# Matmul minus a matrix: transfers of up to eight row tiles in a listed order, through two rings

## The chip, the core and the metric

The kernel runs on one core of a Trainium2 chip. The engines that matter are PE (TensorE, matmuls and transposes by matmul), DVE (VectorE), ACT (ScalarE), SP (which only issues DMA transfers here) and the core's 16 DMA engines, which move data between HBM and the on-chip memory SBUF. Each engine has its own instruction queue and works through it in order; the engines wait for one another through semaphores. PSUM is the memory into which PE writes.

The metric is device time in microseconds (us). Four runs of the kernel before gave 212.73 to 213.39, median 213.12.

## The reference

```python
batch, m, k, n = 16, 512, 1024, 768
x          # (batch, m, k) float32
weight     # (k, n)        float32
sub_value  # (batch, m, n) float32

def reference(x, weight, sub_value):
    return (np.matmul(x, weight) - sub_value).astype(np.float32)
```

Batch and m together are 8192 rows of x. A row of x has 4 KB, a row of `sub_value` or of the output 3 KB. In all 33.6 MB of x, 25.2 MB of `sub_value` and 3.1 MB of weights are read, and 25.2 MB are written.

## The kernel before

**Tiles.** The rows are cut into 64 m tiles of 128 rows, one row to each of the 128 partitions of SBUF. Which row goes where is set by the views `x_s`, `sub_s` and `out_s`: the rows fall into sections of 1024, and in a section partition p holds the S = 8 consecutive rows 8p to 8p + 7. Tile `mi` takes row `mi % 8` of each partition's run in section `mi // 8`. So a transfer of four tiles reads four neighbouring rows for each partition, 16 KB of x or 12 KB of sub in one piece, and the pieces of neighbouring partitions lie 32 KB (x) or 24 KB (sub, out) apart in HBM.

**One tile's way.** ACT casts a tile of x to float16 (`cast`, lines 99 to 108; line 108 for most tiles, 105 for the pairs named below). PE transposes it in four pieces, taking two float16 values as one float32 (`transposes`, line 116), and ACT copies the result out of PSUM (line 123). PE multiplies with the weights in 16 matmuls, four for each of four chunks of k (`matmuls`, line 149). DVE subtracts: `finish` (line 160) reads PSUM and the sub tile and writes the output over the sub tile, from where it is stored. For seven pairs of tiles (18 and 19, 24 and 25, and so on to 54 and 55, `ON_DVE`) DVE does the transpose instead of PE, 16 instructions to a pair (line 137).

**Order.** The program order is written out by hand. A head (lines 186 to 214) does tiles 0 to 2 chunk by chunk as the weights come in, with idle matmuls between. Then a loop over `mi` from 3 to 63 does, in each pass: the transfers (below), the matmuls of tile `mi` with the transposes of tile `mi + 2` between them, the casts of later tiles, `finish(mi)`, and some of the waiting DVE transposes. A tile is cast four passes ahead of its matmuls, a tile of a DVE pair seven passes ahead (`lead`).

**Transfers.** All are issued by SP, in program order. The head's are listed in `HEAD_TRANSFERS`: x and sub one tile at a time at first, then two, with the four weight loads among them. From there on, every fourth pass of the loop issues three transfers of four tiles: a load of x three groups ahead, a load of sub two groups ahead, and the store of the group that was finished two groups ago (lines 220 to 226). After the loop come the last stores: four tiles, then two, one and one (lines 242 to 246).

**Buffers.** A group of four x tiles has a buffer of its own out of four (`x_pool`, 64 KB per partition). A group of four sub tiles, which becomes the output, has one out of seven (`so_pool`, 84 KB per partition); the weights' float32 stages use the same seven. A load into a buffer waits until its previous content is used up: for x until it is cast, for sub until it is stored. Waits are kept by the part of a buffer that an instruction touches: in the profile cast(0) starts when x0 has landed, with loads into other parts of the same buffer under way.

PSUM has two buffers for transposes (`psum_t`) and three for the products (`psum_o`).

Of the kernel before, what the change touches and what calls it, by code (L numbers as in the profile page):

```python
# [8 lines left out]
P = 128  # L9
Q = 32  # L10
F32 = mybir.dt.float32
F16 = mybir.dt.float16

S = 8
G = 4
XA, SA, OA = 3, 2, 2
TA = 2
CA = 2
LEAD_DVE = 7
PER = 4  # L20
HEAD = 3
ON_DVE = frozenset(range(18, 60, 6))
HEAD_TRANSFERS = [('x', 0, 1), ('w', 0, 0), ('x', 1, 1), ('w', 1, 0), ('x', 2, 1), ('w', 2, 0), ('w', 3, 0), ('x', 3, 1), ('s', 0, 1), ('x', 4, 1), ('s', 1, 1), ('x', 5, 1), ('s', 2, 1), ('x', 6, 1), ('s', 3, 1), ('x', 7, 1), ('x', 8, 2), ('s', 4, 2), ('x', 10, 2), ('s', 6, 2)]


@with_exitstack
def kernel(
# [7 lines left out]
    nc = tc.nc  # L35
    keep = tc.keep_in_program_order
# [5 lines left out]
    M_TOT, K = x_flat.shape  # L42
    _, N = weight.shape
    n_mt = M_TOT // P
    n_g = n_mt // G
    NS = N // 2
    KW = K // 2
    n_c = KW // P

    x_s = x_flat.rearrange("(s p j) k -> s p j k", p=P, j=S)  # L50
    sub_s = sub_flat.rearrange("(s p j) n -> s p j n", p=P, j=S)
    out_s = out_flat.rearrange("(s p j) n -> s p j n", p=P, j=S)
    w_c = weight.rearrange("(c p r) n -> c p r n", p=P, r=2)

    def rows(view, mi, n):
        return view[mi // S][:, mi % S : mi % S + n]

    const_pool = ctx.enter_context(tc.tile_pool(name="const", bufs=1))
    w_pool = ctx.enter_context(tc.tile_pool(name="w_pool", bufs=1))
    x_pool = ctx.enter_context(tc.tile_pool(name="x_pool", bufs=4))  # L60
    x16_pool = ctx.enter_context(tc.tile_pool(name="x16_pool", bufs=CA + 2))
    xt_pool = ctx.enter_context(tc.tile_pool(name="xt_pool", bufs=TA + 3))
    x16p_pool = ctx.enter_context(tc.tile_pool(name="x16p_pool", bufs=2))
    xtp_pool = ctx.enter_context(tc.tile_pool(name="xtp_pool", bufs=2))
    so_pool = ctx.enter_context(tc.tile_pool(name="so_pool", bufs=7))
    psum_t_pool = ctx.enter_context(tc.tile_pool(name="psum_t", bufs=2, space=bass.MemoryType.PSUM))
    psum_o_pool = ctx.enter_context(tc.tile_pool(name="psum_o", bufs=3, space=bass.MemoryType.PSUM))

# [3 lines left out]

    w_sb = w_pool.tile([P, n_c, 2, N], F16)

    x_t, so_t, x16_t, xt_t, ps_t, po_t = {}, {}, {}, {}, {}, {}

    def load_w(c):
        st = so_pool.tile([P, 2, N], F32, name="w_stage", tag="so_tile")
        keep(nc.sync.dma_start(out=st, in_=w_c[c]))  # L79
        for r in range(2):  # L80
            keep(nc.vector.tensor_copy(out=w_sb[:, c, r], in_=st[:, r]))  # L81

    def load_x(mi, n):
        g, j = divmod(mi, G)
        if j == 0:
            x_t[g] = x_pool.tile([P, G, K], F32, name="x_tile")
        keep(nc.sync.dma_start(out=x_t[g][:, j : j + n], in_=rows(x_s, mi, n)))  # L87

    def load_sub(mi, n):
        g, j = divmod(mi, G)  # L90
        if j == 0:
            so_t[g] = so_pool.tile([P, G, N], F32, name="so_tile")
        keep(nc.sync.dma_start(out=so_t[g][:, j : j + n], in_=rows(sub_s, mi, n)))

    def store(mi, n):
        g, j = divmod(mi, G)
        keep(nc.sync.dma_start(out=rows(out_s, mi, n), in_=so_t[g][:, j : j + n]))

    def cast(mi):
        g, j = divmod(mi, G)  # L100
        first = mi - mi % 2
        if first in ON_DVE:
            if mi == first:
                x16_t["pair", mi] = x16p_pool.tile([P, 2, K], F16, name="x16p_tile")
            keep(nc.scalar.copy(out=x16_t["pair", first][:, mi - first], in_=x_t[g][:, j]))  # L105
            return
        x16_t[mi] = x16_pool.tile([P, K], F16, name="x16_tile")
        keep(nc.scalar.copy(out=x16_t[mi], in_=x_t[g][:, j]))  # L108


    def transposes(mi):
        def one(c):
            def f():
                if c == 0:
                    ps_t[mi] = psum_t_pool.tile([P, K], F16, name="psum_t")
                keep(nc.tensor.transpose(  # L116
                    ps_t[mi].bitcast(F32)[:, c * P : (c + 1) * P],
                    x16_t[mi].bitcast(F32)[:, c * P : (c + 1) * P],
                    ident,
                ))  # L120
                if c == n_c - 1:
                    xt_t[mi] = xt_pool.tile([P, K], F16, name="xt_tile")
                    keep(nc.scalar.copy(out=xt_t[mi], in_=ps_t.pop(mi)))  # L123
                    x16_t.pop(mi)
            return f
        return [one(c) for c in range(n_c)]

    def transposes_dve(mi):

        x16 = x16_t.pop(("pair", mi)).bitcast(F32).rearrange("p j (c q) -> p (j c) q", c=n_c)  # L130
        xt_p = xtp_pool.tile([P, 2, K], F16, name="xtp_tile")
        xt_t[mi], xt_t[mi + 1] = xt_p[:, 0], xt_p[:, 1]
        xt = xt_p.bitcast(F32).rearrange("p j (c m) -> p (j c) m", c=n_c)

        def one(a, b):
            def f():
                keep(nc.vector.transpose(  # L137
                    xt[b * Q : (b + 1) * Q, :, a * Q : (a + 1) * Q],
                    x16[a * Q : (a + 1) * Q, :, b * Q : (b + 1) * Q],
                ))  # L140
            return f
        return [one(a, b) for a in range(P // Q) for b in range(P // Q)]

    def matmuls(mi, c):
        if c == 0:
            po_t[mi] = psum_o_pool.tile([P, 2, 512], F32, name="psum_o")
        for r in range(2):
            for h in range(2):
                keep(nc.tensor.matmul(  # L149
                    po_t[mi][:, h, :NS],  # L150
                    xt_t[mi][:, 2 * P * c + r : 2 * P * (c + 1) : 2],
                    w_sb[:, c, r, h * NS : (h + 1) * NS],
                    start=(c == 0 and r == 0),
                    stop=(c == n_c - 1 and r == 1),
                ))

    def finish(mi):
        g, j = divmod(mi, G)
        o = so_t[g][:, j].rearrange("p (h n) -> p h n", h=2)
        keep(nc.vector.tensor_tensor(  # L160
            out=o, in0=po_t.pop(mi)[:, :, :NS], in1=o, op=mybir.AluOpType.subtract
        ))


    for kind, at, n in HEAD_TRANSFERS:
        {"w": lambda: load_w(at), "x": lambda: load_x(at, n), "s": lambda: load_sub(at, n)}[kind]()


    idle_w = const_pool.tile([P, P], F16)
# [9 lines left out]
    def lead(mi):  # L179
        return LEAD_DVE if mi - mi % 2 in ON_DVE else TA + CA  # L180
# [4 lines left out]

    idle(13)
    cast(0)
    transpose_tile(0)
    idle(5)
    matmuls(0, 0)  # L190
    cast(1)
    transpose_tile(1)
    idle(4)
    matmuls(0, 1)
    matmuls(1, 0)
    matmuls(1, 1)
    cast(2)
    transpose_tile(2)
    idle(3)
# [6 lines left out]
    for mi in range(HEAD):  # L206
        matmuls(mi, 3)
        finish(mi)
# [7 lines left out]

    waiting = []
    for mi in range(HEAD, n_mt):
        g, j = divmod(mi, G)
        if j == 0 or mi == HEAD:  # L220
            if g + XA < n_g:
                load_x((g + XA) * G, G)
            if g + SA < n_g:
                load_sub((g + SA) * G, G)
            if g >= OA:
                store((g - OA) * G, G)
        t = mi + TA
        tr = transposes(t) if t < n_mt and t - t % 2 not in ON_DVE else []
        for c in range(n_c):
            matmuls(mi, c)  # L230
            if tr:
                tr[c]()
        for t in range(mi, n_mt):
            if t - lead(t) == mi:
                cast(t)
        finish(mi)
        if mi + LEAD_DVE - 1 in ON_DVE:
            waiting += transposes_dve(mi + LEAD_DVE - 1)
        for f in waiting[:PER]:
            f()  # L240
        del waiting[:PER]
    for g in range(n_g - OA, n_g - 1):
        store(g * G, G)
    store(n_mt - G, G - 2)
    store(n_mt - 2, 1)
    store(n_mt - 1, 1)


# [28 lines left out]
```

## Time and profile before

One execution was profiled. It took 212.96 us; the profile's span, from the first to the last instruction, is 211.2 us of it.

| what | value |
|---|---|
| time, median of four runs | 213.12 us |
| time of the profiled execution, its span | 212.96 us, 211.2 us |
| mean granted clock of PE | 0.991 |
| moved between HBM and SBUF | 61.87 MB read, 25.17 MB written |
| transfers issued by SP | 65 |
| matmul of 384 columns (line 149) | 1024 instructions, 326 ns mean, overlapping |
| transposes by PE (line 116) | 200 |
| cast of a tile by ACT (lines 108 and 105) | 64, 1049 and 1046 ns |
| copy of a transposed tile by ACT (line 123) | 50, 1012 ns |
| subtraction by DVE (line 160) | 64, 957 ns |
| transpose by DVE (line 137) | 112, 436 ns |
| last matmul ends, last store issued | 203.9 us, 204.9 us |

Busy time of an engine is what its instructions cover. Matmuls are pipelined, so their times overlap and a busy PE need not be a PE at its peak. The page also divides the span into 40 slices of 5.28 us and gives for each the busy share of every engine and of the DMA engines, in tenths, and the GB/s that were moved. A separate view lists for every line what it waited for, in us in total, in how many cases, and the longest. The chain of waits follows the work that ended last back in time, from each instruction to what released it. For DMA transfers the trace has the time of issue on SP's queue and the time until the data has landed.

### The profile page before, as it was taken

What the parts mean: (1) busy time and instruction counts of PE and PEld (TensorE: products, weight loads), DVE (VectorE), ACT (ScalarE), POOL (GpSimd) and SP (SyncE); (2) the same over time, 40 slices, a digit from 0 to 9 for tenths busy, and PEclk for the clock granted to TensorE, in tenths of its full rate; (3) what the DMA queues carried; (4) which work ended last, traced back from release to release, by engine and by line L of the source; (5) the groups of instructions that cost most, each with busy time, mean ns of one, the idle gap of its engine ahead of it and who ended that gap; (6) DMA issues with size and microseconds to landing.
All of it is one profiled execution on the core that took longest, in us unless ns stands there. A gap on an engine that the chain in (4) does not pass through costs nothing.

```text
span 211.2 us, 3028 instructions
## 1 busy us (share of the span) xinstructions
PE 198.4 (94%) x1249; PEld 130.0 (62%) x1249; DVE 114.1 (54%) x186; ACT 112.6 (53%) x115; POOL 0.7 (0%) x6
## 2 busy tenths in 40 slices
PE   7999799999999999999989999998999999999960
PEld 2465576677666666666656567664656667667630
DVE  0333313152697299399519939942993993242330
ACT  3547666757852846565086555509646453656300
POOL 1000000000000000000000000000000000000000
PEclk9999999999999999999999999999999999999996
DMA  6999999999999999999999999999999999999994
GB/s 217 423 412 391 422 417 446 417 417 441 425 428 417 433 432 414 437 426 431 421 431 434 417 431 429 431 421 432 430 424 433 400 434 414 427 412 431 431 413 182
DMA packets 9374, 87.23 MB, mean 413 GB/s; under 512 B 1040, under 2 KB 1040, under 8 KB 3728
## 3 DMA queue, kind: packets, MB, share of 16 engines
q1 hardware_dynamic: 9360, 87.04, 98.3%
q8 instruction: 10, 0.16, 0.3%
q14 instruction: 4, 0.03, 0.0%
HBM read 61.87 MB, written 25.17 MB: 412 GB/s over the span
## 4 chain that ended last, share of the span: by engine, by line
DMA 49%; PE 33%; ACT 10%; DVE 3%; SPq 2%; issue 1%; ACTq 0%
DMA x_tile<-in_x_dram 49%; PE psum_o L149 28%; PE psum_t L116 5%; ACT x_tile L108 4%; ACT xt_tile L123 3%; ACT x16p_tile L105 2%; DVE xtp_tile L137 2%; DVE so_tile L160 1%; SPq L79 1%; SPq L87 1%; ACTq L105 0%
## 5 line engine op out<-in xcount | busy, mean ns | idle before, releaser
L149 PE MATMUL psum_o<-w_sb,xt_tile 128*128 128x384 f16 x800 | 145.7, 326 | 1.7 <-ACT xt_tile L123 1.6
L149 PEld LDWEIGHTS <-xt_tile 128*128 128x128 f16 x800 | 78.2, 98 | 41.6 <-ACT xt_tile L123 2.7
L160 DVE TENSOR_TENSOR so_tile<-psum_o,so_tile 128x768 f32<-128x768 f32 x64 | 60.8, 957 | 57.2 <-PE psum_o L149 33.7
L123 ACT COPY xt_tile<-psum_t 128x1024 f16<-128x1024 f16 x50 | 50.6, 1012 | 58.9 <-PE psum_t L116 58.2
L137 DVE STREAM_TRANSPOSE xtp_tile<-x16p_tile 32x256 f32<-32x256 f32 x112 | 48.8, 436 | 22.4 <-ACT x16p_tile L105 20.6
L108 ACT CAST x_tile<-x_tile 128x1024 f16<-128x1024 f32 x50 | 51.7, 1049 | 6.7 <-DMA x_tile<-in_x_dram 6.6
L116 PE MATMUL psum_t<-ident,x_tile 128*128 128x128 f32 x200 | 52.4, 274 | 2.0 <-ACT x_tile L108 1.4
L149 PE MATMUL psum_o<-w_sb,xtp_tile 128*128 128x384 f16 x224 | 42.9, 326 | 0.6 <-DVE xtp_tile L137 0.6
L116 PEld LDWEIGHTS psum_t<-ident,x_tile 128*128 128x128 f32 x200 | 27.6, 141 | 16.1 <-ACT x_tile L108 4.3
L149 PEld LDWEIGHTS <-xtp_tile 128*128 128x128 f16 x224 | 21.8, 98 | 10.9 <-DVE xtp_tile L137 1.4
L105 ACT CAST x16p_tile<-x_tile 128x1024 f16<-128x1024 f32 x14 | 14.6, 1046 | 20.9 <-DMA x_tile<-in_x_dram 20.9
L81 DVE CAST w_sb<-w_stage 128x768 f16<-128x768 f32 x8 | 4.1, 556 | 10.3 <-DMA w_stage<-in_weight_dram 10.3
L177 PE MATMUL psum_o<-idle_x,idle_w 128*128 128x512 f16 x25 | 8.4, 493 | 1.3 <-DVE idle_x L172 1.3
L177 PEld LDWEIGHTS <-idle_w 128*128 128x128 f16 x25 | 3.1, 122 | 4.9 <-issue 3.2
L108 ACT ACT_TABLE_LOAD x1 | 1.3, 1283 | 0.7 <-PEq L261 0.7
L171 DVE MEMSET idle_w<- 128x64 uint32 x1 | 0.1, 112 | 0.8 <-PEq L261 0.8
masks.py:199 POOL TENSOR_SCALAR_AFFINE_SELECT ident<-ident 128x128 f32<-128x128 f32 x1 | 0.3, 295 | 0.1
L172 DVE MEMSET idle_x<- 128x256 uint32 x1 | 0.3, 272 | 0.0
masks.py:197 POOL MEMSET ident<- 128x128 f32 x1 | 0.2, 205 | 0.3 <-POOLq L261 0.3
L261 POOL MEMSET const-bfloat16-1.0<- 128x1 bf16 x1 | 0.1, 102 | 0.0
L261 POOL MEMSET const-uint8-127<- 128x1 uint8 x1 | 0.1, 102 | 0.0
L261 POOL MEMSET const-float32-0.0<- 128x1 f32 x1 | 0.1, 99 | 0.2 <-issue 0.2
(1 smaller groups left out, 0.1 us busy)
## 6 DMA issues: line engine op xcount, KB each, us to landing
x_tile<-in_x_dram SPq DMA_DIRECT2D x13, 2048.0 KB, 30.8
out_dram<-so_tile SPq DMA_DIRECT2D x15, 1536.0 KB, 31.7
so_tile<-in_sub_value_dram SPq DMA_DIRECT2D x14, 1536.0 KB, 32.9
x_tile<-in_x_dram SPq DMA_DIRECT2D x8, 512.0 KB, 10.7
w_stage<-in_weight_dram SPq DMA_DIRECT2D x4, 768.0 KB, 8.5
x_tile<-in_x_dram SPq DMA_DIRECT2D x2, 1024.0 KB, 13.0
so_tile<-in_sub_value_dram SPq DMA_DIRECT2D x4, 384.0 KB, 11.8
so_tile<-in_sub_value_dram SPq DMA_DIRECT2D x2, 768.0 KB, 13.6
```

The source lines that it names most:

```text
L79: keep(nc.sync.dma_start(out=st, in_=w_c[c]))
L81: keep(nc.vector.tensor_copy(out=w_sb[:, c, r], in_=st[:, r]))
L87: keep(nc.sync.dma_start(out=x_t[g][:, j : j + n], in_=rows(x_s, mi, n)))
L105: keep(nc.scalar.copy(out=x16_t["pair", first][:, mi - first], in_=x_t[g][:, j]))
L108: keep(nc.scalar.copy(out=x16_t[mi], in_=x_t[g][:, j]))
L116: keep(nc.tensor.transpose(ps_t[mi].bitcast(F32)[:, c * P : (c + 1) * P], x16_t[mi].bitcast(F32)[:, c * P : (c + 1) * P], ident,))
L123: keep(nc.scalar.copy(out=xt_t[mi], in_=ps_t.pop(mi)))
L137: keep(nc.vector.transpose(xt[b * Q : (b + 1) * Q, :, a * Q : (a + 1) * Q], x16[a * Q : (a + 1) * Q, :, b * Q : (b + 1) * Q],))
L149: keep(nc.tensor.matmul(po_t[mi][:, h, :NS], xt_t[mi][:, 2 * P * c + r : 2 * P * (c + 1) : 2], w_sb[:, c, r, h * NS : (h + 1) * NS], start ...
L160: keep(nc.vector.tensor_tensor(out=o, in0=po_t.pop(mi)[:, :, :NS], in1=o, op=mybir.AluOpType.subtract))
L177: keep(nc.tensor.matmul(idle_o[:, 0], idle_w, idle_x, start=True, stop=True))
L261: nc = _bacc.Bacc("TRN2", target_bir_lowering=False, num_devices=1)
```

## The change

The views keep their form, but S is 64 instead of 8: partition p now holds rows 64p to 64p + 63 of x, `sub_value` and the output, and the whole input is one section. Tile `mi` is row `mi` of each partition's run. In HBM the pieces of neighbouring partitions lie 256 KB (x) or 192 KB (sub, out) apart, and a transfer of eight tiles takes 32 KB or 24 KB in one piece for each partition.

The groups of four are gone. One tile of SBUF with 16 slots holds x (64 KB per partition, as before), one with 32 slots holds sub and output (96 KB per partition); tile `mi` sits in slot `mi % 16` or `mi % 32`. The weights' float32 stages use the last eight slots of the second ring.

All transfers stand in one list, `TRANSFERS`, which SP issues in that order. `issue()` is called once at the start and then after every `cast` and every `finish` while the program is built; it places the next entries of the list as long as what they need has been placed: for a load of x the casts of the tiles that had its slots, for a load of sub the stores of those tiles, for a store the finishes of its tiles. On the chip each transfer then waits for these to be done. The list begins with x0, the weights and single tiles, goes on with two to five tiles, and has transfers of eight from sub 8 to 15 on. It has 39 entries.

What is computed, and the order of work on PE, ACT and DVE, stay as they are.

```diff
-S = 8
-G = 4
-XA, SA, OA = 3, 2, 2
+S = 64
+NX, NSO = 16, 32
...
+TRANSFERS = [
+    ('x', 0, 1), ('w', 0, 1), ('x', 1, 1), ('w', 1, 1), ('x', 2, 1), ('w', 2, 1),
+    ('w', 3, 1), ('x', 3, 2), ('s', 0, 1), ('x', 5, 3), ('s', 1, 3), ('x', 8, 3),
+    ('s', 4, 4), ('x', 11, 5), ('s', 8, 8), ('x', 16, 8), ('x', 24, 3), ('s', 16, 8),
+    ('x', 27, 5), ('o', 0, 8), ('s', 24, 8), ('x', 32, 8), ('s', 32, 8), ('o', 8, 8),
+    ('x', 40, 8), ('s', 40, 8), ('x', 48, 8), ('o', 16, 8), ('o', 24, 8), ('s', 48, 8),
+    ('x', 56, 8), ('s', 56, 8), ('o', 32, 8), ('o', 40, 8), ('o', 48, 8), ('o', 56, 4),
+    ('o', 60, 2), ('o', 62, 1), ('o', 63, 1),
+]
...
+    x_ring = x_pool.tile([P, NX, K], F32)
+    so_ring = so_pool.tile([P, NSO, N], F32)
...
+    def issue():
+        while todo:
+            kind, at, n = todo[0]
+            span = set(range(at, at + n))
+            old = {t - NX if kind == "x" else t - NSO for t in span}
+            need, by = {
+                "w": (set(), "o"),
+                "x": ({t for t in old if t >= 0}, "cast"),
+                "s": ({t for t in old if t >= 0}, "o"),
+                "o": (span, "finish"),
+            }[kind]
+            if not need <= done[by]:
+                return
+            todo.pop(0)
+            done[kind] |= span
...
+            here = ring[:, at % size : at % size + n]
+            there = view[at // S][:, at % S : at % S + n]
+            if kind == "o":
+                keep(nc.sync.dma_start(out=there, in_=here))
+            else:
+                keep(nc.sync.dma_start(out=here, in_=there))
...
     def cast(mi):
...
+        issue()
...
     def finish(mi):
...
+        issue()
...
     for mi in range(HEAD, n_mt):
-        g, j = divmod(mi, G)
-        if j == 0 or mi == HEAD:
-            if g + XA < n_g:
-                load_x((g + XA) * G, G)
-            if g + SA < n_g:
-                load_sub((g + SA) * G, G)
-            if g >= OA:
-                store((g - OA) * G, G)
...
-    for g in range(n_g - OA, n_g - 1):
-        store(g * G, G)
-    store(n_mt - G, G - 2)
-    store(n_mt - 2, 1)
-    store(n_mt - 1, 1)
```

More of the change, by code (lines that the diff above doesn't have):

```diff
@@ L22 @@
 ON_DVE = frozenset(range(18, 60, 6))
-HEAD_TRANSFERS = [('x', 0, 1), ('w', 0, 0), ('x', 1, 1), ('w', 1, 0), ('x', 2, 1), ('w', 2, 0), ('w', 3, 0), ('x', 3, 1), ('s', 0, 1), ('x', 4, 1), ('s', 1, 1), ('x', 5, 1), ('s', 2, 1), ('x', 6, 1), ('s', 3, 1), ('x', 7, 1), ('x', 8, 2), ('s', 4, 2), ('x', 10, 2), ('s', 6, 2)]
+TRANSFERS = [
[7 rows of a table added]
+]
 @with_exitstack
@@ L44 @@
     n_mt = M_TOT // P
-    n_g = n_mt // G
     NS = N // 2
@@ L59 @@
     w_pool = ctx.enter_context(tc.tile_pool(name="w_pool", bufs=1))
-    x_pool = ctx.enter_context(tc.tile_pool(name="x_pool", bufs=4))
+    x_pool = ctx.enter_context(tc.tile_pool(name="x_pool", bufs=1))
     x16_pool = ctx.enter_context(tc.tile_pool(name="x16_pool", bufs=CA + 2))
@@ L64 @@
     xtp_pool = ctx.enter_context(tc.tile_pool(name="xtp_pool", bufs=2))
-    so_pool = ctx.enter_context(tc.tile_pool(name="so_pool", bufs=7))
+    so_pool = ctx.enter_context(tc.tile_pool(name="so_pool", bufs=1))
     psum_t_pool = ctx.enter_context(tc.tile_pool(name="psum_t", bufs=2, space=bass.MemoryType.PSUM))
@@ L73 @@
     w_sb = w_pool.tile([P, n_c, 2, N], F16)
[L75 to L83, printed above, removed]
-        g, j = divmod(mi, G)
-        if j == 0:
-            x_t[g] = x_pool.tile([P, G, K], F32, name="x_tile")
-        keep(nc.sync.dma_start(out=x_t[g][:, j : j + n], in_=rows(x_s, mi, n)))
@@ L89, in load_sub @@
[L89 to L97, printed above, removed]
+    x_ring = x_pool.tile([P, NX, K], F32)
+    so_ring = so_pool.tile([P, NSO, N], F32)
+    x16_t, xt_t, ps_t, po_t = {}, {}, {}, {}
@@ new lines @@
+    todo = list(TRANSFERS)
+    done = {"w": set(), "x": set(), "s": set(), "o": set(), "cast": set(), "finish": set()}
+    def issue():
[13 more added lines that the diff above has]
+            done[kind] |= span
+            if kind == "w":
+                first = NSO - 2 * (n_c - at)
+                st = so_ring[:, first : first + 2]
+                keep(nc.sync.dma_start(out=st, in_=w_c[at]))
+                for r in range(2):
+                    keep(nc.vector.tensor_copy(out=w_sb[:, at, r], in_=st[:, r]))
+                continue
+            ring, size, view = {
+                "x": (x_ring, NX, x_s), "s": (so_ring, NSO, sub_s), "o": (so_ring, NSO, out_s)
+            }[kind]
+            here = ring[:, at % size : at % size + n]
[4 more added lines that the diff above has]
+                keep(nc.sync.dma_start(out=here, in_=there))
@@ L99, in cast @@
     def cast(mi):
-        g, j = divmod(mi, G)
+        assert mi in done["x"]
+        done["cast"].add(mi)
+        x_in = x_ring[:, mi % NX]
         first = mi - mi % 2
@@ L104, in cast @@
                 x16_t["pair", mi] = x16p_pool.tile([P, 2, K], F16, name="x16p_tile")
[L105 to L108, printed above, removed]
+            keep(nc.scalar.copy(out=x16_t["pair", first][:, mi - first], in_=x_in))
+        else:
+            x16_t[mi] = x16_pool.tile([P, K], F16, name="x16_tile")
+            keep(nc.scalar.copy(out=x16_t[mi], in_=x_in))
+        issue()
     def transposes(mi):
@@ L157, in finish @@
     def finish(mi):
-        g, j = divmod(mi, G)
-        o = so_t[g][:, j].rearrange("p (h n) -> p h n", h=2)
+        assert mi in done["s"]
+        done["finish"].add(mi)
+        o = so_ring[:, mi % NSO].rearrange("p (h n) -> p h n", h=2)
         keep(nc.vector.tensor_tensor(
@@ L162, in finish @@
         ))
-    for kind, at, n in HEAD_TRANSFERS:
-        {"w": lambda: load_w(at), "x": lambda: load_x(at, n), "s": lambda: load_sub(at, n)}[kind]()
+        issue()
+    issue()
     idle_w = const_pool.tile([P, P], F16)
@@ L218 @@
     for mi in range(HEAD, n_mt):
-        g, j = divmod(mi, G)
-        if j == 0 or mi == HEAD:
-            if g + XA < n_g:
-                load_x((g + XA) * G, G)
-            if g + SA < n_g:
-                load_sub((g + SA) * G, G)
-            if g >= OA:
-                store((g - OA) * G, G)
         t = mi + TA
@@ L241 @@
         del waiting[:PER]
-    for g in range(n_g - OA, n_g - 1):
-        store(g * G, G)
-    store(n_mt - G, G - 2)
-    store(n_mt - 2, 1)
-    store(n_mt - 1, 1)
+    assert not todo
 _INS = ['x', 'weight', 'sub_value']
```

## The prediction

> **What bounds the kernel now.** First the page: span, engines, DMA rate by slice, queue, chain.
>
> ```profile
> span 211.2 us, 3028 instructions
> ...
> PE 198.4 (94%) x1249; PEld 130.0 (62%) x1249; DVE 114.1 (54%) x186; ACT 112.6 (53%) x115; POOL 0.7 (0%) x6
> ...
> GB/s 217 423 412 391 422 417 446 417 417 441 425 428 417 433 432 414 437 426 431 421 431 434 417 431 429 431 421 432 430 424 433 400 434 414 427 412 431 431 413 182
> DMA packets 9374, 87.23 MB, mean 413 GB/s; under 512 B 1040, under 2 KB 1040, under 8 KB 3728
> ...
> q1 hardware_dynamic: 9360, 87.04, 98.3%
> ...
> DMA 49%; PE 33%; ACT 10%; DVE 3%; SPq 2%; issue 1%; ACTq 0%
> ```
>
> Two resources look full, PE at 94% and the DMA queue at 98.3%. The waits tell which one leads:
>
> ```profile
> ACT x16p_tile L105 <- DMA x_tile<-in_x_dram: 20.9, 5, 7.2
> ...
> PE psum_t L116 <- ACT x_tile L108: 1.4, 1, 1.4
> ```
>
> The DVE tiles' casts wait for x five times, up to 7.2 us each; PE itself hardly waits, since it is fed two tiles ahead, which covers most of such a wait. In windows of one round (four m tiles of loads and stores) and at the end, the columns are window, length, busy time of each engine, granted clock, DMA share, GB/s:
>
> ```profile
> 81.70:93.90 12.20, 12.20 (x82) 8.31 (x80) 8.35 (x16) 6.72 (x8) 0.00 (x0) 1.00 1.01 429
> ...
> 106.10:118.30 12.20, 11.33 (x72) 7.18 (x71) 7.99 (x15) 9.52 (x10) 0.00 (x0) 1.00 1.01 429
> ...
> 155.30:167.80 12.50, 12.20 (x80) 8.19 (x79) 8.82 (x17) 6.92 (x7) 0.00 (x0) 1.00 1.01 420
> ...
> 207.00:208.00 1.00, 0.00 (x0) 0.00 (x0) 0.00 (x0) 0.00 (x0) 0.00 (x0) 0.73 0.73 298
> 208.00:209.00 1.00, 0.00 (x0) 0.00 (x0) 0.00 (x0) 0.00 (x0) 0.00 (x0) 0.50 0.39 157
> ```
>
> DMA share is 1.0 while PE drops to 11.33 of 12.20 (and a busy PE is not PE at its peak); at the end the engines run dry one by one. By the chain a quarter of a normal tile is 0.65 + 0.11 us on PE, so a tile is 3.04 us, and 2.60 us where the DVE transposes. A period of six (four normal, two DVE) is 17.4 us, 2.9 us per tile. DMA moves 1.31 MB per tile (4, 3 and 3 KB by 128 partitions), at 429 GB/s 3.05 us. So **the kernel runs at the pace of its DMA queue, with PE 5% behind it**. The span is bytes over rate, plus a start and a tail.
>
> **How long one transfer takes.** Narrowing the DMA view to one issue gives its time to landing; for the last x load the queue's timeline and that view say:
>
> ```profile
> x_tile<-in_x_dram SPq DMA_DIRECT2D x1, 2048.0 KB, 32.0
> ```
>
> Issued at 148.48, landed at 180.5. Done for every issue, differences of successive landings are the price of each transfer (first in, first out). Six rounds from 69.5 to 142.7 us give 4.84 us for four tiles of x, 3.70 for four of sub, 3.66 for four of out, 12.2 together. In the head, x1, x2 and x3 took 1.26, 1.23 and 1.20, and s1 and s3 0.97 and 0.99. From x: a tile is (4.84 - 1.23)/3 = 1.20 us, and a transfer has 0.03 us of its own. From sub: (3.70 - 0.98)/3 = 0.91, and 0.07. I take **0.05 us per transfer**. The page's packets explain where it would sit: 65 transfers with 128 runs each plus 16 completion packets each are 9,360, the queue's number.
>
> **The change, part by part.**
>
> 1. *Fewer, larger transfers.* 65 become 39 with the same bytes: 26 x 0.05 = **1.3 us off the DMA path**, with nothing beside it to hide it, since the DMA path sets the end. Bounds: nothing, if the 0.05 is scatter of landings. Above: per tile (1.21 x, 0.925 sub, 0.915 out) what follows x3's landing at 15.84 is 60 x 1.21 + 64 x 0.925 + 64 x 0.915 = 190.4 us, so 206.2; the last store landed at 210.3. The lost 4.1 us are s2 landing 1.5 us late (22.9, after 20.5 for x5), single transfers, a stretch from 142.7 to 180.5 of 12.6 us per round instead of 12.2 (1.2 us), and the tail. Gain 0 to 4.1; I take 1.3 because it is the part that two sizes in the trace tie to the number of transfers. As a check, the Trainium skill ("DMA: Bandwidth & Descriptors", Where 436 GB/s comes from) has a ceiling of 435 GB/s; the 86.5 MB after x0's landing (4.5 us) would take 198.8 us by it against 205.8 here: no layout gains more than 7.
>
> 2. *The pitch in HBM.* A partition's rows lie 32 KB apart (x) and 24 KB (sub, out) today, 256 and 192 KB afterwards. No row of the trace has such a pitch; the nearest is x at 32 KB, 434 GB/s (2.097 MB in 4.84 us). Here a rule speaks against the change: the same page, Latency and other measured facts, reports copies of 128 rows of 16 KiB that fall from 214 GB/s per direction to 207 at a pitch of 512 KiB and to 164 at 2 MiB. By the row x costs nothing more. By the rule's lightest entry, x's 64 x 1.21 = 77.4 us would grow by 3.3%, 2.6 us. 256 KB is half the smallest pitch that lost anything, and 192 KB is no power of two; I take 0 and keep 2.6 for the range. A gain from longer runs (32 instead of 16 KB) is bounded by 435 against 434 for x: 0.2 us.
>
> 3. *The head.* x3 comes with x4, 1.2 us later (17.05 instead of 15.84), and cast(3) waited for it. Then cast(4) needs no wait; s0 and x5-7 bring x5 at 21.6, where cast(5) started at 21.3. PE is about 1 us later in its first loop pass. The DMA queue sees none of it: its first seven issues are the same. 0 on the path.
>
> 4. *Eight-tile loads and the casts.* At the rows' rates landings afterwards are: s1-3 24.4, x8-10 28.0, s4-7 31.7, x11-15 37.8, s8-15 45.2, x16-23 54.8, s16-23 65.9, x27-31 71.9, o0-7 79.2, x32-39 96.3, o8-15 111.0, x40-47 120.7, s40-47 128.1, x48-55 137.8, o16-23 145.1, o24-31 152.4, s48-55 159.8, x56-63 169.5. cast(18) (line 105) is placed in pass 11 and ran at 51.2; it waits until 54.8, 3.6 us. Behind it in ACT's queue are xt(14), cast(16) and cast(19). xt(14) ran at 52.4, would end at 56.8, and PE needs it for tile 14 at about 55.4: **PE stalls 1.4 us**. Later: 22 tiles to pass 35's end (14 with transposes), 22 x 2.60 + 14 x 0.44 = 63.4, so cast(42) is due at 120.2, x40-47 lands at 120.7. cast(48) due at 137.6, landing 137.8; cast(56) due at 169.7, landing 169.5. All within PE's slack. PE from tile 14 on: 50 x 2.60 + 34 x 0.44 = 145, end at 201.8 against 203.9 now (it no longer has the stalls at 104 and 142 us). Sub: s8-15 at 45.2 makes finish(8) late, but three PSUM buffers carry PE to tile 11 at 46.3. These are stalls of PE, which has some 2.4 us to spare; 0 on the path.
>
> 5. *The queue's waits.* SP is in order: each entry waits, and all behind it too. x48-55 needs cast(39), at pass 35's end (120.2): on an empty queue it would land 2.6 us later plus its 9.7 (x0: issue 0.74, landing 4.53, less 1.2 of data), so 132.5; the queue's turn gives 137.8. Margin 5.3. s48-55 needs o16-23 landed at 145.1: 145.1 + 2.6 + 7.4 = 155.1 against 159.8, margin 4.7. s32-39 needs o0-7 (79.2), turn 96.3 on: ample. x16-23 needs cast(7) near 28 us, turn 45.2. So the DMA engines don't run dry. The wait of an issue for the landing of the eighth before it, seen in the head (x4 issued at 6.42, w0 landed at 6.4), holds more bytes in flight with larger transfers. 0.
>
> 6. *Tail.* The last stores keep their sizes (two tiles, one, one). Now the last is issued at 204.9 behind a backlog and lands 5.4 us later. With PE's end at 201.8 it is issued near 203, the backlog again decides.
>
> Sum: span 211.2 - 1.3 = 209.9. Around it lie 212.96 - 211.2 = 1.76 us, so 211.7 for this execution; the median is 0.16 above it: **211.8 us**.
>
> **The rivals.** A measurement of this kernel tells about 0.3% (0.6 us) from no change.
>
> - *A, forecast, 0.52:* 210.0 to 212.4.
> - *B, nothing saved, 0.16.* The engines' share is 1.0 whatever the transfer, the rate is near 435 already, and 0.05 us is small against landings that scatter by 0.1. Against it: both x and sub show it with its sign. 213.1.
> - *C, the pitch, 0.18.* Streams of x spaced at a power of two slow each other. For it: the rule, and that x is 39% of the bytes. Against: the spare between 207 and 214 is small at twice this pitch. Price 2.6 - 1.3 = +1.3: 214.4; it decides from a loss of 1.7% of x. If sub and out shared it (117.8 us x 3.3% = 3.9), 218.3.
> - *D, lumps, 0.14, slower.* Casts in ACT's order stop at each eight-tile load (18, 42, 48, 56), and the slack doesn't cover it. PE's end then sets the time: a lone 384 KB store lands 3.8 us after issue like x0 did, so PE must end by 209.0 - 3.8 - 1.0 = 204.2, 2.4 us after plan. At 7 us of added stall (twice 3.5) PE ends at 208.8, the span is 213.6, the time 215.5, and x48-55 eats its margin. Against it: the due times above agree within 0.5 us.
>
> The range 210.0 to 215.5 holds A, B and most of C and D. Faster 0.52, same 0.16, slower 0.32.
>
> **What would show it.** Queue packets 39 x 144 = 5,616 (one per run of 32 KB); DMA share still 1.0 throughout; eight tiles of x land in 9.6 to 9.7 us (over 9.9 speaks for C); ACT's wait of cast(18) near 3.6 us and PE's end near 202; no slice with DMA below 9 (D). Wrong would be: a rate below 425 in the middle with the share at 1.0, or a DMA share under 1.0 between 120 and 160 us.

## The result, and the profile after

The kernel after takes 212.49 us in the median (211.55 to 213.05), the kernel before beside it 212.93: ratio 0.9974, 95% interval 0.9967 to 0.9980. That is 0.44 us by the medians, some 0.5 us by the ratio, where 1.3 us had been forecast. The profiled execution took 212.87 us, so it lies above its median.

First the page of the kernel after: span, engines, DMA per slice, packets, the transfers' queue, and the chain by engine.

```profile
span 211.1 us, 2967 instructions
...
PE 197.6 (94%) x1249; PEld 130.1 (62%) x1249; DVE 114.1 (54%) x186; ACT 112.9 (53%) x115; POOL 0.7 (0%) x6
...
DMA  6999999999999999999999999999999999999982
...
DMA packets 5629, 87.22 MB, mean 413 GB/s; under 512 B 624, under 2 KB 624, under 8 KB 2032
...
q1 hardware_dynamic: 5616, 87.03, 97.2%
...
PE 68%; DMA 19%; ACT 4%; DVE 3%; SPq 2%; issue 1%
```

The packets are the 5,616 of the prediction, so the transfers have the form that the change says. Two things are new. The queue's share is 97.2% instead of 98.3%: 1.1% of 211 us, so on the mean each of the 16 engines worked some 2.3 us less. And the chain, which ran through DMA for 49% before, now runs through PE for 68%. Had one only these two numbers, one would say that the saving was made and that PE took the DMA queue's place.

The waits of ACT and PE agree with that reading. ACT's casts for the DVE tiles wait 7.7 us for x instead of 20.9, and all but 0.3 us of PE's own waits lie in the first 60 us.

```profile
ACT x16p_tile L132 <- DMA x_ring<-in_x_dram: 7.7, 3, 3.0
...
PE psum_t L144 <- ACT x_tile L135: 3.1, 3, 1.4
```

Then the last microseconds, in windows of one (busy time of PE, its weight loads, DVE, ACT and GpSimd, then granted clock, DMA share, GB/s):

```profile
204.00:205.00 1.00, 0.25 (x2) 0.00 (x0) 0.71 (x1) 0.00 (x0) 0.00 (x0) 1.00 0.78 320
205.00:206.00 1.00, 0.00 (x0) 0.00 (x0) 0.25 (x1) 0.00 (x0) 0.00 (x0) 1.00 0.56 230
206.00:207.00 1.00, 0.00 (x0) 0.00 (x0) 0.00 (x0) 0.00 (x0) 0.00 (x0) 1.00 0.94 378
207.00:208.00 1.00, 0.00 (x0) 0.00 (x0) 0.00 (x0) 0.00 (x0) 0.00 (x0) 1.00 0.26 105
208.00:209.00 1.00, 0.00 (x0) 0.00 (x0) 0.00 (x0) 0.00 (x0) 0.00 (x0) 1.00 0.13 52
209.00:210.00 1.00, 0.00 (x0) 0.00 (x0) 0.00 (x0) 0.00 (x0) 0.00 (x0) 0.77 0.08 31
```

In the kernel before, one of these windows was:

```profile
205.00:206.00 1.00, 0.00 (x0) 0.00 (x0) 0.00 (x0) 0.00 (x0) 0.00 (x0) 1.00 0.98 409
```

The last store is issued at 205.28 us and lands at 210.19. Between 205 and 206 nearly half of the DMA engines have run dry (share 0.56, before 0.98). After 208 a share of 0.13 and 0.08 is the work of two engines and of one, of 16 (1/16 is 0.06). So most engines have the saved time, but a transfer has landed only when its slowest engine is done. Which it is, the trace doesn't name.

The differences of successive landings show where these engines fell behind. In us, for some transfers of the kernel after (x40-47 is the load of tiles 40 to 47 of x, s stands for sub, o for the output); the second column is the median of its kind in this kernel, for s1-3 three times a tile's 0.92:

| transfer | usual | after |
|---|---|---|
| s1-3 | 2.8 | 4.17 |
| s32-39 | 7.4 | 7.59 |
| x40-47 | 9.7 | 10.16 |
| x48-55 | 9.7 | 9.84 |
| s56-63 | 7.4 | 8.09 |
| o32-39 | 7.3 | 8.73 |

Three theories were tested; the second and the third can hold together. **PE**: its end at 204.3 us holds back the last stores. **Slow engine**: one DMA engine's backlog sets the last landing. **Pitch**: the 256 and 192 KB between the partitions' pieces took back what fewer transfers gave (rival C of the prediction).

### The profile page after: what moved, and what is told of

Its sections match the earlier page's. It is cut to its first block, busy times and chain, and to the rows that moved or that the text cites. A ratio compares the mean times of both kernels' runs of the same rounds, so it can differ in the third digit from the quotient of the medians.

```text
span 211.1 us, 2967 instructions
## 1 busy us (share of the span) xinstructions
PE 197.6 (94%) x1249; PEld 130.1 (62%) x1249; DVE 114.1 (54%) x186; ACT 112.9 (53%) x115; POOL 0.7 (0%) x6
## 3 DMA queue, kind: packets, MB, share of 16 engines
q1 hardware_dynamic: 5616, 87.03, 97.2%
## 4 chain that ended last, share of the span: by engine, by line
PE 68%; DMA 19%; ACT 4%; DVE 3%; SPq 2%; issue 1%
PE psum_o L177 60%; DMA x_ring<-in_x_dram 19%; PE psum_t L144 8%; ACT x_tile L135 2%; DVE xtp_tile L165 2%; ACT xt_tile L151 1%; DVE so_ring L189 1%; SPq L110 1%; SPq L122 1%; ACT x16p_tile L132 0%
## 5 line engine op out<-in xcount | busy, mean ns | idle before, releaser
L189 DVE TENSOR_TENSOR so_ring<-psum_o,so_ring 128x768 f32<-128x768 f32 x64 | 60.7, 957 | 62.5 <-PE psum_o L177 41.3
L135 ACT CAST x_tile<-x_ring 128x1024 f16<-128x1024 f32 x50 | 51.6, 1048 | 7.1 <-DMA x_ring<-in_x_dram 7.1
L132 ACT CAST x16p_tile<-x_ring 128x1024 f16<-128x1024 f32 x14 | 14.6, 1046 | 7.7 <-DMA x_ring<-in_x_dram 7.7
L112 DVE CAST w_sb<-so_ring 128x768 f16<-128x768 f32 x8 | 4.1, 557 | 10.2 <-DMA so_ring<-in_weight_dram 10.2
L205 PE MATMUL psum_o<-idle_x,idle_w 128*128 128x512 f16 x25 | 7.7, 461 | 1.3 <-DVE idle_x L200 1.3
```

The source lines that it names most:

```text
L112: keep(nc.vector.tensor_copy(out=w_sb[:, at, r], in_=st[:, r]))
L135: keep(nc.scalar.copy(out=x16_t[mi], in_=x_in))
L189: keep(nc.vector.tensor_tensor(out=o, in0=po_t.pop(mi)[:, :, :NS], in1=o, op=mybir.AluOpType.subtract))
L205: keep(nc.tensor.matmul(idle_o[:, 0], idle_w, idle_x, start=True, stop=True))
```

## The experiments

**PE made shorter.** In tiles 24 to 59 the matmuls of the last k chunk take half their columns; the other half of that chunk's product is left out. The number of instructions stays.

```diff
+        w = NS // 2 if c == n_c - 1 and 24 <= mi < 60 else NS
...
-                    po_t[mi][:, h, :NS],
+                    po_t[mi][:, h, :w],
...
-                    w_sb[:, c, r, h * NS : (h + 1) * NS],
+                    w_sb[:, c, r, h * NS : h * NS + w],
```

In the kernel after:

> The kernel after, with the four matmuls of the last k chunk in tiles 24 to 59 at half their columns (192 instead of 384; the other half of that chunk's product is left out). Transfers, their order and the number of instructions are those of the kernel after; PE has about 36 x 4 x 0.08 = 11.5 us less to do. Theory PE (from 59 us on PE runs without a wait and its end at 204.3 us holds back the last stores): the last store is issued before 202 us and the time falls by 1.5 us or more against the kernel after, ratio to before 0.991 or less. Theory slow engine (15 of the 16 DMA engines have the saved time, but one has more to do and its backlog sets the last landing): PE ends earlier, yet the last landing stays within 0.5 us of 210.2, ratio 0.995 to 0.999.

In the kernel before:

> The same shortening of tiles 24 to 59 in the kernel before (same part left out). It shows how much of the time before was PE's. Theory PE: the kernel before was paced by its DMA queue, so 0 to 0.6 us, ratio 0.997 to 1.000; the difference to the short-PE run of the kernel after is what the change takes off the DMA path, 1 us or more. Theory slow engine: also 0.997 to 1.000, but the difference between the two short-PE runs is under 0.7 us.

Measured: 0.9971 (0.9963 to 0.9980) for the kernel after, against 0.9974 unshortened, and 0.9998 (0.9987 to 1.0009) for the kernel before. The last store was issued at 203.69 us, only 1.6 earlier, since the casts now waited for x (up to 6.3 us at once) and PE behind them. It landed at 209.65, half a us earlier, in an execution that was as much shorter (212.32 us against 212.87). Its windows, of the shortened kernel after:

```profile
202.00:203.00 1.00, 0.67 (x5) 0.20 (x2) 0.30 (x1) 0.00 (x0) 0.00 (x0) 1.00 0.90 378
...
208.00:209.00 1.00, 0.00 (x0) 0.00 (x0) 0.00 (x0) 0.00 (x0) 0.00 (x0) 0.50 0.07 28
209.00:210.00 1.00, 0.00 (x0) 0.00 (x0) 0.00 (x0) 0.00 (x0) 0.00 (x0) 0.50 0.02 6
```

PE ends in the window from 202, and the tail of one engine is still there. Theory PE falls for this kernel, although 68% of the chain lies on PE: a chain names the last releaser, not how close the second was.

**The pitch undone.** One number:

```diff
-S = 64
+S = 8
```

> The kernel after with S = 8: rings and list as they are, but partitions lie 32 KB (x) and 24 KB apart in HBM as before, and each transfer of eight reads one solid block. Theory pitch (the 256 KB and 192 KB pitch took back the saving): 1 us or more faster than the kernel after, ratio to before 0.993 or less, and eight tiles of x land in under 9.65 us each. Theories PE and slow engine: no difference to the kernel after, ratio 0.9955 to 0.9990.

Measured: 211.12 us (211.00 to 211.16, five executions), ratio 0.9913 (0.9899 to 0.9926). That is 1.9 us faster than the kernel before and 1.4 us faster than the kernel after. Two more pairs below that differ in S alone agree: with PE shortened 0.9971 against 0.9893, with a head of small transfers 1.0001 against 0.9938. The same windows with S = 8, whose last store is issued at 205.26 us, as in the kernel after:

```profile
204.00:205.00 1.00, 0.23 (x2) 0.00 (x0) 0.73 (x1) 0.00 (x0) 0.00 (x0) 1.00 0.75 304
205.00:206.00 1.00, 0.00 (x0) 0.00 (x0) 0.23 (x1) 0.00 (x0) 0.00 (x0) 1.00 0.34 138
206.00:207.00 1.00, 0.00 (x0) 0.00 (x0) 0.00 (x0) 0.00 (x0) 0.00 (x0) 1.00 0.94 375
207.00:208.00 1.00, 0.00 (x0) 0.00 (x0) 0.00 (x0) 0.00 (x0) 0.00 (x0) 0.67 0.16 62
208.00:209.00 1.00, 0.00 (x0) 0.00 (x0) 0.00 (x0) 0.00 (x0) 0.00 (x0) 0.50 0.00 0
```

The store lands 3.0 us after its issue instead of 4.9. Landings tell where the 1.9 us between these two profiles arose: s32-39 7.29 (0.30 less), x40-47 9.65 (0.51), x48-55 9.71 (0.13), s56-63 7.30 (0.79). s1-3 (4.17) and o32-39 (8.57) are about as late as with S = 64, so these two have another cause. Theory pitch holds in sign and size. The expectation that eight tiles of x would land in under 9.65 us was too sharp: they take 9.57 to 9.80.

**Which pitch, and how far.** First x alone at S = 64, then sub and out alone (the rows that meet in the subtraction don't belong together), then S = 32 for all:

```diff
-S = 64
+SX, SO = 64, 8
```

> The kernel after with x at S = 64 (256 KB pitch) and sub and out at S = 8 (24 KB pitch, solid blocks). Rows of x and sub_value that don't belong together meet in the subtraction. Theory power of two (x's pitch is the costly one): as the kernel after, ratio to before 0.9965 to 0.9985. Rival, sub and out (192 KB; 58% of the bytes, and all writes): as the kernel after with S = 8, 0.990 to 0.993. If both share it: 0.993 to 0.996.

> The counterpart: x at S = 8 (32 KB pitch), sub and out at S = 64 (192 KB). Again rows that don't belong together meet. Theory power of two: as the kernel after with S = 8, ratio 0.990 to 0.993. Rival, sub and out: 0.9965 to 0.9985. If both share it: 0.993 to 0.996.

> The kernel after with S = 32: pitch 128 KB (x) and 96 KB (sub, out). Theory pitch with a steep start (a cost only at the largest pitches): ratio 0.990 to 0.993, as with S = 8. If the cost grows evenly with the pitch: about half of it, 0.993 to 0.996. If any gap between the partitions' pieces costs (only S = 8 makes a transfer of eight one solid block): 0.9965 to 0.9985.

| kernel | pitch x / sub, KB | median us | ratio to before (95%) |
|---|---|---|---|
| after | 256 / 192 | 212.49 | 0.9974 (0.9967 to 0.9980) |
| x alone wide | 256 / 24 | 211.96 | 0.9951 (0.9937 to 0.9965) |
| sub and out alone wide | 32 / 192 | 212.13 | 0.9955 (0.9938 to 0.9971) |
| S = 32 | 128 / 96 | 211.57 | 0.9935 (0.9918 to 0.9952) |
| S = 8 | 32 / 24 | 211.12 | 0.9913 (0.9899 to 0.9926) |

Both share the cost. 192 KB, no power of two, costs about as much as 256 KB. S = 32 lies between; by the intervals it is told from S = 64, but not from either single pitch, nor surely from S = 8. S = 8 also makes a transfer of eight tiles one solid block of HBM. At S = 32 there are gaps as at S = 64, at a smaller cost, so gaps alone don't explain the 1.4 us; how much of it they have is not shown.

**The pitch in the kernel before.** The same edit the other way, S = 64 in the kernel before:

> The kernel before with S = 64 instead of 8 and nothing else: transfers of up to four tiles as before, but partitions 256 KB (x) and 192 KB apart. Theory pitch (the pitch by itself costs about 1.4 us, as the kernel after gains that much when it is undone): slower than before by 1.0 to 1.8 us, ratio 1.004 to 1.008, with landings that come late at some transfers. Rival, pitch only with runs of 32 KB: no change, ratio 0.9985 to 1.0015, as the runs are 16 KB here.

Measured: 213.37 us, ratio 1.0017 (1.0009 to 1.0026). Slower, but by 0.4 us, between what the two theories gave room for. Beside 65 transfers the pitch costs a third of what it costs beside 39.

**A head of small transfers.** The list up to x23 as in the kernel before, 48 transfers, so that PE isn't late in the first 60 us; once with S = 64, once with S = 8:

```diff
-    ('w', 3, 1), ('x', 3, 2), ('s', 0, 1), ('x', 5, 3), ('s', 1, 3), ('x', 8, 3),
-    ('s', 4, 4), ('x', 11, 5), ('s', 8, 8), ('x', 16, 8), ('x', 24, 3), ('s', 16, 8),
+    ('w', 3, 1), ('x', 3, 1), ('s', 0, 1), ('x', 4, 1), ('s', 1, 1), ('x', 5, 1),
+    ('s', 2, 1), ('x', 6, 1), ('s', 3, 1), ('x', 7, 1), ('x', 8, 2), ('s', 4, 2),
+    ('x', 10, 2), ('s', 6, 2), ('x', 12, 4), ('s', 8, 4), ('x', 16, 4), ('s', 12, 4),
+    ('x', 20, 4), ('x', 24, 3), ('s', 16, 8),
```

> The kernel after with the first transfers as small as before (x, sub tile by tile, then two and four up to x23, 48 transfers in all), the rest of the list unchanged. PE should lose no time in the first 60 us: cast(18) doesn't wait, PE reaches tile 14 at about 55.5 us instead of 58. Theory PE: the last store is issued 1.5 to 2.5 us earlier than in the kernel after (205.3), and the time falls by 1 us or more, ratio to before 0.993 or less. Theory slow engine: PE gains early and waits later for x40 to x47 and x56 to x63; the last landing doesn't move earlier, ratio 0.997 to 1.000 (nine more transfers cost up to 0.5 us).

> The kernel after with S = 8 and the fine head of the earlier run (48 transfers). With S = 8 the last store was issued at 205.3 us and landed after only 3.0 us on engines that had run dry, so PE sets the end there. Theory PE at S = 8: the fine head brings the last store forward by about 1 us (204.2 with the fine head at S = 64 against 205.3), ratio to before 0.986 to 0.990. Rival, the DMA queue still sets the end and nine transfers more cost 0.05 us each: 0.991 to 0.995.

Measured: 1.0001 (0.9988 to 1.0014) with S = 64 and 0.9938 (0.9920 to 0.9957) with S = 8. Both are about 0.0026 over the same kernel with 39 transfers, 0.5 us for nine transfers or 0.06 each. The last store was issued earlier (204.24 and 203.56 us), which again bought nothing. With S = 8, PE shortened as above:

> The kernel after with S = 8 and the last k chunk of tiles 24 to 59 at half its columns (the other half of that product is left out), so PE has 11.5 us less to do. Theory PE at S = 8: the DMA engines stood idle for about 2 us in sum before the last landing, so the time falls by 0.6 to 1.6 us against S = 8 alone, ratio to before 0.984 to 0.989. Rival, the DMA queue sets the end: as S = 8 alone, 0.990 to 0.993. The ratio against the short-PE run of the kernel before (0.9998) is what fewer and larger transfers take off the DMA path: by the prediction 1.3 us.

210.90 us, 0.9893 (0.9874 to 0.9912): between the two theories, and not told from S = 8 alone. The profiles decide: the last store was issued 4.4 us earlier (200.84 us) and landed at 208.42, against 208.28. So there too the DMA engines set the end and not PE. Against the shortened kernel before (213.00) the shorter list at S = 8 is worth 2.1 us.

**The transfers alone.** All casts, matmuls and subtractions are left out, and sub goes out as it came in; SP issues the list, each transfer when its slots' earlier transfers have landed.

> The list of the kernel after with its transfers alone: no casts, matmuls or subtractions, so sub goes out as it came in and the products are left out. SP issues each transfer when the slots' earlier transfers have landed. S = 64. Theory pitch: slower than the same at S = 8 by 1 to 2 us, with late landings at some transfers and a tail in which one or two engines work. Rival, the pitch costs only beside the traffic and the order that the compute engines cause: equal within 0.5 us.

> The same transfers alone with S = 8. Theory pitch: 1 to 2 us faster than with S = 64, 16 engines ending together. By the spacing of landings in the kernels, 87 MB at 430 to 435 GB/s: a span near 206 us. Rival: as S = 64 within 0.5 us.

> The 65 transfers in the order of the kernel before (up to four tiles) alone, S = 8, no computation (products and subtraction left out). Against the 39 transfers alone at S = 8 (208.4 us). Theory of the prediction's step 1 (0.05 us per transfer): 26 x 0.05 = 1.3 us more, 209.7 us, 209.2 to 210.2. Rival, the saving is not in the number of transfers: within 0.4 us of 208.4.

Medians: 208.44 us with S = 64, 208.43 with S = 8, and 212.36 for the 65 transfers of the kernel before. Two surprises. The pitch costs nothing that can be seen here (four executions of each, one of them with S = 8 at 209.56 us; by the intervals at most 0.5 us). And the list of 65 costs 3.9 us more than the list of 39, 0.15 for each transfer, three times the prediction's term. The two lists also mix loads and stores differently, and in the trace it is mostly stores among loads that take longer than in the kernel before (o0-3 4.40 us, o4-7 4.24, against some 3.7 there). So the 0.15 belongs to this pair of lists; that the number alone costs so much is not shown.

The kernel at S = 8 takes 2.7 us more than its transfers alone. The trace of the kernel after, in the 1 us window from 21 us, shows something that the transfers alone don't have:

```profile
q1 hardware_dynamic: 57, 0.42, 101.2%
q8 instruction: 1, 0.02, 6.9%
```

It is a fetch of instructions, 16 KB in one packet. 6.9% of 16 engines for 1 us are 1.1 us of one engine. There are ten of them, some 20 us apart. The first, at 21 us, comes just ahead of s1-3, which lands 1.4 us late; the ninth, in the window from 182 us, just ahead of o32-39, late by as much:

```profile
q8 instruction: 1, 0.02, 6.0%
```

Alone, these two took 2.78 and 7.30 us.

**The transfers beside an instruction stream.** 1150 idle matmuls that touch none of the data bring the fetches back. In the first try they had 430 columns:

> The 39 transfers alone at S = 64, and beside them 1150 idle matmuls (2300 PE instructions, as many as in the kernels) that touch none of the data; the reference's arithmetic is left out. They bring back the instruction fetches, 16 KB each on one DMA engine, that the transfers-alone kernel didn't have. Theory fetch: landings come about 1.4 us late after the first fetch near 21 us and again after the ninth near 182 us, and the time is 2 to 3 us over that of the transfers alone (208.4). Theory pitch beside fetches (the wider pitch costs only where an engine has lost time to a fetch): 0.8 us or more over the same at S = 8. Rival, pitch beside the compute engines' own traffic or the kernels' waits: equal to S = 8 within 0.5 us.

> The same at S = 8. Theory fetch: 210.4 to 211.4 us, near the short-PE run at S = 8 (210.9), with the two late landings of about 1.4 us. Rival, fetches cost nothing: 208.4.

These gave 215.67 and 214.76 us, but the stream itself ended last (PE works beyond 212 us in both profiles), so these times say nothing of the transfers. Their landings do: o60-61 at 206.09 us with S = 64 and at 205.19 with S = 8. With 384 columns PE is done before 200 us:

```diff
+    for _ in range(IDLE):
+        keep(nc.tensor.matmul(idle_o[:, 0, :384], idle_w, idle_x[:, :384], start=True, stop=True))
```

> The 39 transfers at S = 64 beside 1150 idle matmuls of 384 columns (0.16 us each, 185 to 190 us in all), so that the PE stream ends well before the transfers and the time is theirs; products and subtraction are left out. In the longer stream the stream itself set the time, and only the landings could be compared (o60 to o61 at 206.0 us with S = 64, 205.2 with S = 8). Theory pitch beside fetches: 0.6 us or more over the same at S = 8. Rival, no such effect: within 0.3 us of S = 8.

> The same at S = 8. Theory fetch: 1.4 us (one late landing near 21 us) to 2.8 us (a second one near 180 us) over the transfers alone at 208.4, so 209.8 to 211.2. Rival, fetches cost nothing: 208.4.

> The 65 transfers in the order of the kernel before at S = 8 beside the same stream. Alone they took 212.4 us, 3.9 more than the 39, that is 0.15 us for each transfer and not 0.05. If the fetches' cost adds to that: 213.8 to 215.2. If a fetch's delay is taken up by the waits that the many transfers cause anyway (the kernel before, with all its compute, takes 212.9): 212.3 to 213.3, and the number of transfers is then worth about 2 us beside fetches.

| transfers | alone | beside the stream | the kernel with this list |
|---|---|---|---|
| 39, S = 8 | 208.43 | 210.82 (210.74 to 210.94) | 211.12 |
| 39, S = 64 | 208.44 | 210.92 (210.82 to 211.88) | 212.49 |
| 65, S = 8 | 212.36 | 212.63 (212.27 to 213.31) | 212.93 |

The queues of the 39 transfers with S = 8 beside the stream, and of the same 39 alone with S = 64:

```profile
q1 hardware_dynamic: 5616, 87.03, 97.9%
q8 instruction: 9, 0.15, 0.3%
```

```profile
q1 hardware_dynamic: 5616, 87.03, 98.9%
```

Nine fetches, 0.3% of the engines' time, make the 39 transfers 2.4 us longer. In the profile of this run x5-7 lands after 4.94 us instead of 3.7, following the fetch at 19 us, and o40-47 after 7.93 instead of 7.3, following the ninth at 185 (s48-55 is late there too, 7.95, with no fetch close before it). Beside 65 transfers the same stream costs 0.3 us. **These losses don't add.** So fewer transfers are worth 3.9 us alone and 1.8 us beside fetches (0.07 each), and this 1.8 is what the kernel with S = 8 has gained (1.9).

The pitch is explained by the fetches in part at most. Beside the stream S = 64 and S = 8 differ by 0.1 us in the median (by the intervals at most 0.8), though one of six executions with S = 64 took 211.88, and in the first try o60-61 landed 0.9 us apart. The whole 1.4 us appear only with the kernel's own compute.

**Engine by engine.** The trace has sixteen marks for every landing (624 for the 39 transfers), read here as one for each DMA engine; they carry times and no names. The last mark is the landing. For o60-61, in one execution of each, in us (the profiled one of the 39 alone with S = 8 was that of 209.56 us, so S = 64 stands for them):

| run | first mark | ninth | last |
|---|---|---|---|
| kernel before | 205.30 | 206.61 | 208.40 |
| kernel after | 203.53 | 205.26 | 208.34 |
| kernel after with S = 8 | 203.11 | 204.78 | 206.43 |
| 39 alone, S = 64 | 203.03 | 203.66 | 203.85 |
| 39 beside the stream, S = 8 | 203.05 | 204.75 | 206.23 |
| 65 alone, S = 8 | 205.40 | 206.49 | 207.99 |
| 65 beside the stream, S = 8 | 204.77 | 206.36 | 208.20 |

The change brought the first engine forward by 1.8 us and the last by 0.06. With S = 8 one mark lies over 1.2 us behind the first after the first fetch, two after the second, and so on to seven after the seventh (at o16-23): each fetch put another engine behind, and the landing stayed as late as after one. The ninth came to an engine that was already behind: the last mark trailed the first by 1.91 us before it (s56-63) and by 3.24 after it (o32-39). In the first try of the stream with S = 8 the ninth came at 206 us, and o60-61 landed 1.0 us earlier than in the second. That is why only the first and the ninth show in the landings.

The pitch put a few engines further back. In the kernel after, no mark is over 2.5 us behind the first up to o8-15, one is at x40-47, three at x48-55 (with S = 8 none before the ninth fetch), while the number over 1.2 us stays at that of the fetches: they are engines that fetches had already put behind. The 65 transfers alone drift apart without fetch or wide pitch, by 2.6 us against 0.8 for the 39; of the 4.1 us between these two landings, 2.4 are at the first mark too, 0.09 for each transfer.

## Why the prediction was wrong

- **Step 2, the pitch, failed.** It put "0 and keep 2.6 for the range", because 256 KB is half the smallest pitch that lost anything in the page it cites (the Trainium skill, "DMA: Bandwidth & Descriptors", Latency and other measured facts), and 192 KB is no power of two. With S as the only difference the runs show 1.4 us, three quarters of what the shorter list had gained, and sub and out bear as much of it as x. Rival C, at 0.18, named the right cause, but not how it works: a pitch that is no power of two costs as much, and in the transfers alone no loss shows. The pitch even passed its point ("it decides from a loss of 1.7% of x", 1.3 us), but against a saving of 1.9 us instead of 1.3, so the sum stayed on the faster side. The prediction had named the sign to look for, eight tiles of x over 9.9 us, and one of five shows it (10.16).
- **Step 1, fewer transfers, had the right sign and was too small in size.** The term 26 x 0.05 = 1.3 us measures 1.8 beside fetches and 3.9 alone. Why the spacing of landings gave too little is argued and not shown: it is the pace of the engine furthest behind, and misses what the others lose meanwhile. It would fit that the six rounds take 12.2 us each in the kernel before and 12.4 in the same 65 transfers alone. Two readings that the term rests on were exchanged: four tiles of sub take 3.66 us and four of out 3.70, which makes sub's own term 0.09 instead of 0.07 and leaves the sum as it is. Of the 4.1 us that the step listed as lost, s2's 1.5 are the fetch at 20.6 us: fifteen of its marks come by 21.47, the last at 22.90. No step had the fetches.
- Together: 1.9 gained less 1.4 lost is the 0.5 that was measured. With S = 8 the forecast of 211.8 would have been 0.7 us too high.
- **Step 3 and step 4** were off in the details. PE reached its end at 204.3 us and not at 201.8: the head's later x and the late s1-3 cost about 2 us by pass 4 (the copy of tile 6 starts at 30.19 us, 28.09 before), and cast(18) waited 3.0 us (3.6 predicted). The conclusion, nothing on the path, held: with 11.5 us less work on PE the time stays the same.
- **Step 5, the queue's waits,** held: s48-55 was issued at 147.33 us, right after o16-23 had landed, and landed at 161.85 in its turn.
- **Step 6** said the backlog decides the end. It does, but it is the backlog of one or two engines, while most of the 16 had already run dry.
- Rival B (nothing saved) is refuted by the 65 transfers against the 39. Rival D came in part, as stalls of PE in the first 62 us, and had no price.

Open: why the pitch costs its full 1.4 us only in the whole kernel, and why it falls on engines that were already behind. The transfers with the stream lack the casts', subtractions' and copies' traffic in SBUF and the waits for compute in SP's queue; these were not tried one by one. Whether the ninth fetch comes to the very engine of the first is not shown, as the marks have no names.

The version to keep is the new list and rings with S = 8: 211.12 us.

## What to carry to other kernels

When a queue of 16 engines is the bound, the time is that of the engine furthest behind: look at how the DMA share falls in the last microseconds, not only at its mean. Price a list of transfers by running it alone, since here the spacing of landings inside the kernel understated it; then expect to see only part of it, because delays on different engines overlap. A change of layout that comes with a change of size is a change of its own: try them apart, here it was one number.

## What the runs showed of the hardware

- 65 transfers in place of 39 of the same bytes, in a finer mix of loads and stores, cost 3.9 us with nothing else running (212.36 against 208.43 us), and 1.8 us beside instruction fetches (212.63 against 210.82).
- A fetch of 16 KB of instructions takes about 1.1 us of one DMA engine; nine of them stretch 39 transfers by 2.4 us (208.43 to 210.82). The first seven fall on seven different engines (marks of the kernel after with S = 8).
- Partitions 256 and 192 KB apart instead of 32 and 24 KB cost 1.4 us of 212 in this kernel (0.9974 against 0.9913), and no such loss shows in the transfers alone (208.44 against 208.43).
